# An explicit list schedule for every engine and DMA queue in a two-block transformer kernel

## The chip, the cores and the metric

The kernel runs on one core of a Trainium2 chip. The metric is device time of one execution in microseconds (us), the median of three runs. The engines named below are TensorE (PE, with PEld for its weight loads), VectorE (DVE), ScalarE (ACT), GpSimd (POOL) and SyncE (SP), whose queue issues most DMAs.

## The reference

Sequence length is 512 tokens, width 1024, one batch, all in float32. Five stages run one after the other on a residual stream `h`:

```
# layer A
q, k, v = split(rms_norm(h) @ a_w_qkv)              # 8 heads, two 64-wide halves each, v 128 wide
a       = softmax(q_c . k_c / 8 + t5_bias, causal)  # for each half c
o       = (a[0] - lam * a[1]) @ v
h      += (rms_norm(o) * (1 - lam_init)) @ a_w_o
h      += conv_gated_ffn(h);  h += ple(h)           # 2 x 2816 hidden; conv over 3 tokens
# layer B
k_nope, k_pe, v, q = latent projections, norms, rotary   # 16 heads, 128 + 64 wide
h      += causal_attention(q, k, v) @ b_w_o
h      += conv_gated_ffn(h);  h += ple(h)
# mixer: sparse attention (three branches), conformer convolution, chunked gated linear attention
z       = rms_norm(h) @ w_in
h      += concat(y_nsa, y_conv, y_gla) @ w_out
h      += (silu(x @ w_gate) * (x @ w_up)) @ w_down;  h += ple(h)
out     = rms_norm(h)
```

## The kernel before

All dense products are made of three: each float32 operand is split into a rounded high part and a rest, and `mm3` (L285 records every matmul) adds high x rest, high x high and rest x high in PSUM. A weight piece of 128 x 1024 values or less is loaded by SP into one of two raw buffers (`wr`, RB = 2, L378), ACT writes its high part `wh`, and DVE its rest `wl`, with a gain multiplied in where a norm stands ahead; four such pairs exist (`weight`, tags `wr`, `wh`, `wl`). `X` is the normed activation, transposed and split in the same way. PSUM has four `acc` banks for products over the weights, two `tr` banks for transposes and attention output, and two `s` banks for scores. L295 records every transpose, and L148 every operation on DVE, ACT and POOL.

Layer A works on two heads at a time: projections "p0 v0 p1 p2 p3 v1" (`A_ORDER`), the splits of q and k (`qs`, `kh`, `kl`) from `tr`, then for each head and 128-token tile the scores, a masked softmax (`sb`, `nm`), the transpose of the weights (`wT`) and the product with `v`. `sub_norm` normalizes attention output (`on`), and the last projection uses `a_w_o`. Layer B projects four groups of heads and runs attention per head; a bias row table (`rel_rows`, `tb` and `oh`, L537 on) for the mixer is made near its start. The mixer projects in `MIX_ORDER`, and the gated linear attention (tags `gst`, `gA`) walks its chunks in sequence. Each feed-forward stage holds the token tiles and streams the weights.

The order of work is set in two steps. Stages are coroutines that an `Order` object steps through by rank and by a rough clock (`Engine.slot`: 70 + 1.05 ns per word on DVE, 190 + 0.75 on ACT, 350 + 1.0 on POOL); that gives the order in which instructions are written. The framework's scheduler then orders each engine's instructions with its own timeline model (`schedule_with_timeline_sim=True` in `kernel`). The result is one fixed list of instructions for each engine.

Of the kernel before, what the change touches and what calls it, by code (L numbers as in the profile page):

```python
# [2 lines left out]

# [1 line left out]

# [6 lines left out]
F32 = mybir.dt.float32  # L12
# [20 lines left out]
FAC = 1.0  # L33
MIX_ORDER = "conv b gla k q0 kv a q1 q2 q3"
SL = 1.0
D = 1024
EPS = 1e-6
LAM_INIT = 0.8 - 0.6 * math.exp(0.0)
# [30 lines left out]
class Flag:  # L69


    def __init__(self):
        self.done = False
# [101 lines left out]
        self.used -= k  # L175


class Normed:


# [4 lines left out]
class Model:  # L185
    def __init__(self, ctx, tc, I, O):
        self.tc, self.I, self.O = tc, I, O
        self.n, self.rings = 0, {"acc": [], "tr": [], "s": []}
        self.od, self.g = Order(), {}
        nc = self.nc = Issue(self.od, tc.nc)  # L190
        self.acc, self.wu, self.xs, self.cr, self.sl = Slots(4), Slots(WB), Slots(2), Slots(3), Slots(2)
        pool = lambda name, **k: ctx.enter_context(tc.tile_pool(name=name, **k))
        self.cp = pool("cp", bufs=1)
        self.hp = pool("hp", bufs=1)
        self.wp = pool("wp", bufs=4)
        self.st = pool("st", bufs=4)
        self.sc = pool("sc", bufs=2)
        self.ps = pool("ps", bufs=2, space=bass.MemoryType.PSUM)
        self.dp = pool("dp", bufs=1, space=bass.MemoryType.DRAM)

        self.ident = self.cp.tile([P, P], F32, name="ident", tag="ident")
        make_identity(tc.nc, self.ident)
        self.mhalf = self.cp.tile([P, 32], F32, name="mhalf", tag="mhalf")
        nc.gpsimd.memset(self.mhalf, -0.5)
        self.h = self.hp.tile([P, NT, D], F32, name="h", tag="h")

        self.X = [self.hp.tile([P, 8, S], F32R, name=f"X{i}", tag=f"X{i}") for i in range(2)]
# [5 lines left out]
        return [y[:, k, c0:c0 + n] for y in self.X]  # L213

    def phase(self, name, bufs=1, **k):
        return self.tc.tile_pool(name=name, bufs=bufs, reuse_waits="tile", **k)

    def uid(self, s):
        self.n += 1
# [378 lines left out]
    def bias_a(self, B, fi):  # L598
# [5 lines left out]
        with self.phase("pos") as pp:  # L604
            T = lambda shape, dt, tag: pp.tile(shape, dt, name=self.uid(tag), tag=tag)
            parts = lambda raw, shape, tag="": self.pos_parts(T, raw, shape, tag)
            v = tc.nc.values_load(fi[0:1, 0:1], engines=[EV, EP, ES], min_val=0, max_val=1)
            thr = t5_thresholds()
            nc = self.tc.nc
            with tc.If(v != 0):  # L610
# [10 lines left out]
                for qt in range(NT):  # L621
# [10 lines left out]
                    for h0 in range(0, 8, 2):  # L632
                        for a in acc:
                            nc.vector.memset(a[:, :n], 0.0)
                        for b in range(32):
                            nc.vector.tensor_scalar(eq[:, :n], idx[:, :n], float(b), None, op0=ALU.is_equal)
                            for i, a in enumerate(acc):
                                nc.vector.scalar_tensor_tensor(
                                    a[:, :n], eq[:, :n], tab[:, b * 8 + h0 + i:b * 8 + h0 + i + 1], a[:, :n],
                                    op0=ALU.mult, op1=ALU.add)  # L640
                        for i, a in enumerate(acc):
                            nc.gpsimd.affine_select(
                                out=a[:, :n], in_=a[:, :n], pattern=[[-1, n]], base=qt * P,
                                channel_multiplier=1, compare_op=ALU.is_ge, fill=NEG)
                            nc.gpsimd.dma_start(self.skew(B[h0 // 2][qt + 1], 384 - qt * P, n)[i], a[:, :n])
        return v


# [1283 lines left out]
def model(ctx: ExitStack, tc: tile.TileContext, I, O):  # L1932
# [6 lines left out]
    def nxt(name):  # L1939
        def go(pp=None):  # L1940
# [11 lines left out]
    m.ffn_ple(*at["f2"], *m.glu_ffn(), g["ffn_norm_g_2", 0], I["p_2"][0][0], I["ple_w_gate_2"][0],  # L1952
              I["ple_w_proj_2"][0], g["ple_norm_g_2", 0], m.last_norm, "f2")
    m.od.run()


# [28 lines left out]
```

## Time and profile before

| quantity | value |
|---|---|
| median of three runs | 2270.28 us (2268.73 to 2272.74) |
| the profiled execution | 2270.06 us |
| its span in the trace | 2268.3 us |
| mean granted TensorE clock | 0.988 of full speed |
| PE, DVE, ACT, POOL busy | 97%, 59%, 47%, 8% of the span |

The span is 1.8 us shorter than the execution that it was taken from. Layer A lies at about 10 to 285 us, its feed-forward block at 285 to 684, layer B at 684 to 1140, its block at 1140 to 1482, the mixer at 1482 to 1881, and the last block from 1881 on. A stretch in which PE is busy without a gap can be shortened only by less work or a faster clock; a stretch with gaps can be shortened by giving PE something else to do, or by making what it waits for earlier.

### The profile page before, as it was taken

The page shows a single profiled execution, that of the slowest core. Times are in us where ns is not written, and L with a number is a line of the kernel's source. Part 1 is how long each engine was busy: PE and PEld are TensorE (multiplying, and loading weights), DVE is VectorE, ACT ScalarE, POOL GpSimd, SP SyncE. Part 2 cuts the span into 40 slices and gives each one's busy share as a digit, 9 for nine tenths or more (in the row PEclk, how much of TensorE's full clock was granted, in tenths as well). Part 3 has the DMA queues.
Part 4 walks back from the last instruction along what each step waited for, and adds up shares of the span by engine and source line. Part 5 has one row for each costly group of instructions (what it writes and reads, how often), then busy time and mean ns, then how long its engine had stood idle before and what let it go on. Part 6 is the DMA issues. An engine that isn't in the chain of part 4 may idle for free.

```text
span 2268.3 us, 30282 instructions
## 1 busy us (share of the span) xinstructions
PE 2197.4 (97%) x11166; PEld 1861.9 (82%) x11166; DVE 1336.6 (59%) x2885; ACT 1062.0 (47%) x2102; POOL 173.0 (8%) x232
## 2 busy tenths in 40 slices
PE   7987999999999999999999999999999999999998
PEld 5866798888887888888988888889978888888886
DVE  6668656446545777767565366357977643333344
ACT  4547445334444565555454254254657543323333
POOL 3123000000001121210000000001010000000000
PEclk9999999999999999999999999999989999999999
DMA  6323123332332412212133233234430123323322
GB/s 190 99 63 93 59 84 98 103 98 84 107 98 80 128 43 59 68 40 82 54 107 102 94 103 97 79 98 122 99 91 22 54 66 101 99 91 99 99 89 82
DMA packets 168839, 200.01 MB, mean 88 GB/s; under 512 B 19201, under 2 KB 123709, under 8 KB 168688
## 3 DMA queue, kind: packets, MB, share of 16 engines
q1 hardware_dynamic: 165172, 194.77, 28.1%
q10 hardware_dynamic: 2940, 2.02, 0.3%
q0 software_dynamic: 576, 1.26, 0.3%
q8 instruction: 88, 1.44, 0.3%
q14 instruction: 63, 0.52, 0.1%
HBM read 195.87 MB, written 7.38 MB: 90 GB/s over the span
## 4 chain that ended last, share of the span: by engine, by line
PE 91%; DVE 4%; ACT 1%; DMA 1%; issue 1%; POOL 0%; DVEq 0%; POOLq 0%; SPq 0%; ACTq 0%
PE acc L285 82%; PE s L285 4%; PE tr L295 4%; PE tr L285 1%; DVE wl L148 1%; DVE sb L148 1%; PE s L295 0%; DVE ss L148 0%; DVE X L148 0%; ACT wh L148 0%; DMA xn<-biasB 0%; DVE qs L148 0%; ACT wT L148 0%; DVE qn L148 0%; DMA tb<-rel_bias 0%
## 5 line engine op out<-in xcount | busy, mean ns | idle before, releaser
L285 PE MATMUL acc<-X,wh 128*128 128x512 f32 (+1 forms) x2592 | 734.9, 370 | 4.0 <-DVE X L148 4.0
L285 PEld LDWEIGHTS acc<-X,wh 128*128 128x128 f32 x2592 | 469.9, 189 | 85.0 <-DVE X L148 4.7
L285 PE MATMUL acc<-wh,X 128*128 128x512 f32 (+4 forms) x1664 | 502.0, 380 | 0.2 <-DVE X L148 0.2
L285 PE MATMUL acc<-X,wl 128*128 128x512 f32 (+1 forms) x1296 | 474.7, 369 | 0.0
L148 ACT ACTIVATE wh<-wr,gcol 128x512 fp32r<-128x512 f32 (+5 forms) x480 | 289.6, 656 | 208.4 <-PE acc L285 123.8
L148 DVE SCALAR_TENSOR_TENSOR wl<-wr,gcol,wh 128x512 fp32r<-128x512 f32 (+5 forms) x480 | 306.1, 674 | 131.5 <-ACT wh L148 129.5
L285 PEld LDWEIGHTS acc<-wh,X 128*128 128x128 f32 x1664 | 309.9, 190 | 45.9 <-DVE X L148 0.7
L285 PE MATMUL acc<-wl,X 128*128 128x512 f32 (+4 forms) x832 | 322.4, 388 | 7.3 <-DVE qn L148 3.3
L285 PEld LDWEIGHTS acc<-X,wl 128*128 128x128 f32 x1296 | 244.2, 189 | 40.8
L148 DVE TENSOR_TENSOR wl<-wr,wh 128x1024 fp32r<-128x1024 f32 (+1 forms) x134 | 152.5, 1144 | 183.8 <-ACT wh L148 183.6
L148 POOL TENSOR_TENSOR ss<-ss,mhalf 128x1 f32<-128x1 f32 (+3 forms) x140 | 128.9, 923 | 1727.4 <-DVE ss L148 1703.0
L148 ACT ACTIVATE wh<-wr 128x1024 fp32r<-128x1024 f32 (+1 forms) x134 | 132.5, 995 | 238.9 <-PE acc L285 191.2
L285 PE MATMUL acc<-wh,hh 128*128 128x512 f32 x528 | 205.7, 390 | 0.0
L285 PE MATMUL acc<-wl,hh 128*128 128x512 f32 x528 | 204.5, 389 | 0.0
L285 PE MATMUL acc<-wh,hl 128*128 128x512 f32 x528 | 203.7, 390 | 0.0
L285 PEld LDWEIGHTS acc<-wl,X 128*128 128x128 f32 x832 | 158.1, 190 | 32.8 <-DVE qn L148 3.6
L148 DVE SCALAR_TENSOR_TENSOR cv<-acc,cw,cv 128x511 f32<-128x511 f32 (+1 forms) x176 | 126.1, 745 | 95.2 <-ACT cv L148 94.4
L148 DVE TENSOR_TENSOR h<-h,acc 128x512 f32<-128x512 f32 x120 | 81.6, 684 | 61.3 <-PE acc L285 60.8
L285 PEld LDWEIGHTS acc<-wl,hh 128*128 128x128 f32 x528 | 99.1, 188 | 20.5
L285 PEld LDWEIGHTS acc<-wh,hl 128*128 128x128 f32 x528 | 99.1, 188 | 20.4
L285 PEld LDWEIGHTS acc<-wh,hh 128*128 128x128 f32 x528 | 99.1, 188 | 20.4
L148 ACT ACTIVATE wT<-tr 128x128 f32<-128x128 f32 (+3 forms) x160 | 68.8, 435 | 91.4 <-PE tr L295 90.6
(312 smaller groups left out, 2688.5 us busy)
## 6 DMA issues: line engine op xcount, KB each, us to landing
wr<-ffn_w_in SPq DMA_DIRECT2D x160, 256.0 KB
wr<-ffn_w_out SPq DMA_DIRECT2D x40, 512.0 KB
wr<-ple_w_gate SPq DMA_DIRECT2D x24, 512.0 KB
wr<-ffn_w_gate SPq DMA_DIRECT2D x40, 256.0 KB
wr<-ffn_w_up SPq DMA_DIRECT2D x40, 256.0 KB
wr<-ffn_w_down SPq DMA_DIRECT2D x20, 512.0 KB
wr<-a_w_qkv SPq DMA_DIRECT2D x32, 256.0 KB
wr<-b_w_o SPq DMA_DIRECT2D x16, 512.0 KB
```

Source lines behind the costliest of these rows:

```text
L148: return fn(*args, **kw)
L285: self.nc.tensor.matmul(out, lhsT=a, rhs=b, start=start, stop=stop)
L295: self.nc.tensor.transpose(out, src, self.ident[:src.shape[0], :src.shape[0]])
```

## The change

Every tile pool is wrapped so that each tile's pool and tag are known (`Pool`). After all instructions are traced, `Sequence.graph` builds a dependence graph over them: reads and writes of SBUF by overlapping boxes, PSUM by bank, buffer reuse by `share`. `cost` gives each instruction a time in which its engine is taken and a time until its result is there. `place` is list scheduling: it steps time forward, and whenever an engine is free it takes, of the instructions that are ready, the one with the lowest rank. A first pass ranks by the order as written; then twice (`PASSES = 2`) a pass backward over the program gives how late each instruction can begin, and a pass forward ranks by that. `run` chains each engine's instructions in the order found, by dependences without semaphores. What stands ahead of a branch in `bias_a` (the start of the program) keeps its order.

```diff
+    def cost(i, engine, dma, ins, outs):
+        words = lambda a: math.prod(n for _, n in a.ap[1:])
+        n = max([words(a) for a in ins + outs] or [1])
+        if dma:
+            return 410.0, 1700.0 + 2.1 * n
+        if engine == "PE":
+            n = words(ins[0])
+            f32 = ins[0].dtype == F32 and not any(a.tensor.name.startswith("ident") for a in ins)
+            if f32:
+                return max(223.0, n / 1.2 + 30.0), 175.0 + 1.66 * n
+            pitch = max(110.0, n / 2.4 + 13.6)
+            return pitch, pitch + 162.0
...
+    def place(self, ops, rank, back=False):
...
+            at, e = best
+            due(e, at)
+            k = heapq.heappop(now[e])[1]
+            (pitch, took), first, tab = ops[k][3], ops[k][5], ops[k][6]
+            if tab and tab != table and not back:
+                at, table = at + (1280.0 if table else 0.0), tab
+            free[e] = at + pitch
+            begin[k] = free[e] if back else at
+            order[e].append(k)
...
+    def run(self):
+        ops = self.graph()
+        order, begin = self.place(ops, range(len(ops)))
+        for _ in range(PASSES):
+            _, late = self.place(ops, [-t for t in begin], True)
+            order, begin = self.place(ops, [-t for t in late])
+        for e in self.ENGINES:
+            seq = [ops[k][0] for k in order[e] if not ops[k][5]]
+            for x, y in zip(seq, seq[1:]):
+                self.tc.add_manual_dep(y, x.name, mybir.DependencyInfo(
+                    mybir.DependencyClass.NoSync, mybir.DependencyReason.DATA), reason="order")
...
-        pool = lambda name, **k: ctx.enter_context(tc.tile_pool(name=name, **k))
+        pool = lambda name, **k: ctx.enter_context(self.sq.pool(name, **k))
...
     m.od.run()
+    m.sq.run()
```

The instructions themselves stay the same, but for ACT's table loads (15 in the order of before, 17 now, the two more in the mixer). Of PE's 10580 matmuls 5444 stand elsewhere, by 9 places on average and 213 at most; on SP 217 of 637 DMAs moved, by 1.6 places on average. In layer A the mean shift on PE is 22 to 42 places, in the mixer up to 32, and in the feed-forward blocks no move is over 24 places. The DVE order has a mean shift of 11 places; ACT's is nearly unchanged.

The line numbers of the changed kernel are larger (matmul L509, transpose L519, the helper L150). Three places follow; a number behind a name is one buffer.

PE in layer A before, at the end of the v1 projection (`acc_3762`): the transposes of the last q and k heads (`tr_3783`, `tr_3810`) stand behind it.

```order
L285 MATMUL acc_3762<-wh_3866,X_84 128x512
L295 MATMUL tr_3783<-ident,qn_3717 128x128 x4
L285 MATMUL s_3985<-kh_3013,qs_3012 128x512
L285 MATMUL s_3985<-kl_3014,qs_3012 128x512
L295 MATMUL tr_3810<-ident,qn_3751 128x128 x4
L295 MATMUL tr_3889<-ident,sb_3464 128x128
L295 MATMUL tr_3893<-ident,sb_3482 128x128
L285 MATMUL tr_3900<-v_3758,wT_3891 128x128
```

PE there now:

```order
L509 MATMUL acc_3759<-wh_3826,X_84 128x512
L519 MATMUL tr_3783<-ident,qn_3717 128x128 x4
L509 MATMUL acc_3760<-wl_3827,X_83 128x512
L509 MATMUL acc_3760<-wh_3826,X_83 128x512
L509 MATMUL acc_3760<-wh_3826,X_84 128x512
L509 MATMUL acc_3760<-wl_3827,X_83 128x512
```

The first transpose moved 73 places ahead, from 725 to 652, the second from 728 to 664, and the products of v1 (`acc_3759` to `acc_3762`) now stand between and behind them, up to row 749.

DVE in layer A before: `qs` and `kl` are the splits of those transposes, `wl_3965`, `wl_4332` and `wl_4338` weight splits for `a_w_o`, `on` and `ss` parts of `sub_norm`.

```order
L148 TENSOR_TENSOR wl_3965<-wr_3963,wh_3964 128x1024
L148 SCALAR_TENSOR_TENSOR kl_3425<-tr_3733,gcol_196,kh_3424 64x2x128
L148 TENSOR_TENSOR wl_4332<-wr_4330,wh_4331 128x1024
L148 SCALAR_TENSOR_TENSOR qs_3423<-tr_3783,gcol_196,qs_3423 64x2x128
L148 TENSOR_REDUCE ss_4000<-on_3998 128x4
L148 TENSOR_SCALAR ss_4000<-ss_4000 128x4
L148 TENSOR_TENSOR wl_4338<-wr_4336,wh_4337 128x1024
L148 SCALAR_TENSOR_TENSOR qs_3423<-tr_3810,gcol_196,qs_3423 64x2x128
L148 TENSOR_REDUCE ss_4014<-on_4012 128x4
L148 TENSOR_TENSOR on_3998<-o_2556,ss_4000 128x512
L148 SCALAR_TENSOR_TENSOR kl_3425<-tr_3783,gcol_196,kh_3424 64x2x128
L148 SCALAR_TENSOR_TENSOR kl_3425<-tr_3810,gcol_196,kh_3424 64x2x128
```

DVE there now:

```order
L150 SCALAR_TENSOR_TENSOR qs_3423<-tr_3810,gcol_196,qs_3423 64x2x128
L150 SCALAR_TENSOR_TENSOR qs_3423<-tr_3783,gcol_196,qs_3423 64x2x128
L150 SCALAR_TENSOR_TENSOR rat_3652<-z_3538,nlam,rz_3651 128x1
L150 TENSOR_REDUCE ss_4000<-on_3998 128x4
L150 SCALAR_TENSOR_TENSOR kl_3425<-tr_3810,gcol_196,kh_3424 64x2x128
L150 SCALAR_TENSOR_TENSOR kl_3425<-tr_3783,gcol_196,kh_3424 64x2x128
L150 SCALAR_TENSOR_TENSOR sb_3536<-sb_3536,rat_3652 128x256
L150 TENSOR_TENSOR on_3969<-o_2372,ss_3971 128x512
L150 SCALAR_TENSOR_TENSOR qs_3423<-tr_3810,gcol_196,qs_3423 64x2x128
L150 TENSOR_SCALAR ss_4000<-ss_4000 128x4
L150 TENSOR_TENSOR wl_3959<-wr_3957,wh_3958 128x1024
L150 SCALAR_TENSOR_TENSOR kl_3425<-tr_3810,gcol_196,kh_3424 64x2x128
```

The first split of `tr_3783` moved from 1954 to 1941, and its second `kl` from 1967 to 1959; of the weight splits `wl_3965` moved to 1969, `wl_4332` to 1995 and `wl_4338` to 2013.

PE at the start of layer B before: `tr_7988` and `tr_7991` are the two products of `rel_rows` with the table `tb`, `acc_8100` and `acc_8057` a projection.

```order
L285 MATMUL acc_8100<-wl_8051,X_83 128x320
L285 MATMUL acc_8100<-wh_8050,X_83 128x320
L285 MATMUL acc_8100<-wh_8050,X_84 128x320
L285 MATMUL tr_7988<-oh_7985,tb_7982 8x512
L285 MATMUL tr_7991<-oh_7985,tb_7982 8x128
L295 MATMUL tr_8143<-ident,xn_7900 128x128 x4
```

PE there now:

```order
L509 MATMUL acc_8100<-wh_8034,X_84 128x320
L509 MATMUL tr_7988<-oh_7985,tb_7982 8x512
L509 MATMUL acc_8100<-wl_8043,X_83 128x320
L509 MATMUL acc_8100<-wh_8042,X_83 128x320
L509 MATMUL acc_8100<-wh_8042,X_84 128x320
L509 MATMUL tr_7991<-oh_7985,tb_7982 8x128
L509 MATMUL acc_8100<-wl_8043,X_83 128x320
```

`tr_7988` now stands ahead of the last 12 products of `acc_8100` and not behind them. The DMA that fills `tb` stands at row 474 of ACT's order (470 before).

PE in the mixer before: the last projection of queries (`acc_16696`) ends, and small products of the gated linear attention and of the sparse attention follow without a projection until row 7278.

```order
L285 MATMUL acc_16696<-X_83,wh_16675 128x512
L285 MATMUL acc_16696<-X_83,wl_16676 128x512
L295 MATMUL tr_16631<-ident,cln 128x128 x2
L285 MATMUL acc_16715<-gst_15926,gq 128x256
L295 MATMUL tr_16636<-ident,cln 128x128 x2
L285 MATMUL s_16729<-hs_16169,w_16163 128x64 x2
L285 MATMUL s_16754<-w_16244,hs_16727 128x64 x4
L285 MATMUL tr_16712<-diag,gs_16007 128x512
L285 MATMUL tr_16717<-gv,gs_16083 128x256
```

PE there now:

```order
L509 MATMUL acc_16696<-X_84,wh_16675 128x512
L509 MATMUL acc_16696<-X_83,wh_16675 128x512
L509 MATMUL tr_16712<-diag,gs_16007 128x512
L509 MATMUL acc_16696<-X_83,wl_16676 128x512
L509 MATMUL acc_16696<-X_84,wh_16675 128x512
L509 MATMUL acc_16696<-X_83,wh_16675 128x512
L509 MATMUL tr_16717<-gv,gs_16083 128x256
L509 MATMUL acc_16696<-X_83,wl_16676 128x512
L509 MATMUL acc_16715<-gst_15926,gq 128x256
L509 MATMUL acc_16696<-X_84,wh_16675 128x512
L509 MATMUL acc_16696<-X_83,wh_16675 128x512
```

The products of `acc_16696` are spread between the small ones, from row 7136 to 7199; rows 7200 to 7282 still hold no projection.

## Rows read from the trace of the kernel before

**Rows 1.** The page: busy us of each engine, share, instructions

```profile
PE 2197.4 (97%) x11166; PEld 1861.9 (82%) x11166; DVE 1336.6 (59%) x2885; ACT 1062.0 (47%) x2102; POOL 173.0 (8%) x232
```

**Rows 2.** Windows: stretch, its us, busy us (instructions) per engine, granted clock, DMA share, GB/s

```profile
0.00:57.00 57.00, 41.09 (x193) 31.96 (x194) 36.59 (x81) 27.16 (x50) 22.28 (x27) 1.00 0.63 189
57.00:285.00 228.00, 201.47 (x1019) 166.12 (x1018) 160.69 (x431) 124.10 (x290) 44.98 (x52) 0.95 0.26 78
171.00:228.00 57.00, 45.83 (x232) 37.39 (x232) 49.54 (x125) 40.37 (x93) 19.16 (x23) 0.91 0.32 93
285.00:684.00 399.00, 399.00 (x1888) 334.97 (x1887) 220.17 (x321) 173.12 (x261) 4.88 (x8) 1.00 0.31 96
684.00:741.00 57.00, 52.86 (x257) 44.18 (x256) 31.84 (x69) 24.77 (x49) 8.44 (x14) 0.97 0.28 80
741.00:1140.00 399.00, 394.78 (x2292) 345.30 (x2292) 280.59 (x795) 220.27 (x506) 65.00 (x74) 1.00 0.23 69
1140.00:1482.00 342.00, 342.00 (x1523) 283.43 (x1522) 185.04 (x264) 141.66 (x212) 2.20 (x4) 1.00 0.31 98
1482.00:1539.00 57.00, 54.68 (x277) 46.17 (x276) 31.71 (x52) 28.35 (x47) 7.54 (x22) 1.00 0.35 108
1539.00:1881.00 342.00, 333.84 (x2050) 297.05 (x2049) 238.16 (x659) 193.00 (x484) 13.30 (x24) 0.98 0.26 72
1881.00:2223.00 342.00, 342.00 (x1527) 283.52 (x1526) 128.65 (x182) 113.78 (x173) 2.20 (x4) 1.00 0.31 98
2223.00:2280.00 57.00, 35.69 (x158) 29.23 (x156) 23.12 (x40) 15.82 (x32) 2.21 (x4) 0.94 0.15 56
```

**Rows 3.** The chain of waits: start us, us, what

```profile
330.11 332.78 PE acc L285 x1468
...
730.85 4.32 DMA tb<-rel_bias
```

**Rows 4.** Timeline of PE: start us, us, instruction, idle before and its releaser

```profile
208.31 0.60 PE L295 MATMUL tr<-ident,qn 128*128 128x128 f32 x4
217.40 0.85 PE L295 MATMUL tr<-ident,sb 128*128 128x128 f32 x2 [8.48 <-DVE kl L148]
```

**Rows 5.** Timeline of DVE at the same place

```profile
207.82 1.23 DVE L148 TENSOR_TENSOR wl<-wr,wh 128x1024 fp32r<-128x1024 f32 x1 [1.37 <-ACT wh L148]
...
214.92 0.89 DVE L148 SCALAR_TENSOR_TENSOR qs<-tr,gcol,qs 64x256 fp32r<-64x256 f32 x2
...
216.76 0.90 DVE L148 SCALAR_TENSOR_TENSOR kl<-tr,gcol,kh 64x256 fp32r<-64x256 f32 x2
```

**Rows 6.** Windows of 10 us

```profile
210.00:220.00 10.00, 2.60 (x9) 2.16 (x10) 8.88 (x20) 6.11 (x15) 4.07 (x6) 0.58 0.33 106
1570.00:1580.00 10.00, 10.00 (x53) 9.25 (x52) 10.00 (x28) 6.56 (x18) 0.00 (x0) 1.00 0.53 150
1680.00:1690.00 10.00, 8.91 (x40) 6.84 (x39) 8.89 (x45) 4.12 (x17) 1.29 (x2) 0.64 0.00 0
1690.00:1700.00 10.00, 9.09 (x35) 7.00 (x36) 6.06 (x31) 5.10 (x20) 1.32 (x2) 0.68 0.01 2
```

**Rows 7.** Timeline of PE at the start of layer B

```profile
731.51 0.46 PE L285 MATMUL acc<-wh,X 128*128 128x320 f32 x2
...
731.95 0.46 PE L285 MATMUL acc<-wh,X 128*128 128x320 f32 x2
735.31 1.23 PE L285 MATMUL tr<-oh,tb 33*8 33x512 f32 x4 [2.90 <-DMA tb<-rel_bias]
```

**Rows 8.** ACT's table loads

```profile
L148 ACT ACT_TABLE_LOAD x15 | 19.2, 1283 | 1.6 <-PEq L1975 1.4
```

**Rows 9.** Waits of PE: us in total, times, longest

```profile
PE s L285 <- DVE nm L148: 6.9, 11, 1.6
```

**Rows 10.** Timeline of PE in layer B, score products

```profile
909.17 1.02 PE L285 MATMUL s<-kT,qT 128*128 128x512 f32 x2
...
910.50 0.81 PE L285 MATMUL s<-kT,qT 128*128 128x384 f32 x2
```

More of the change, by code (lines that the diff above doesn't have):

```diff
@@ L1 @@
+import heapq
 import math
-from contextlib import ExitStack
+from contextlib import ExitStack, contextmanager
 import numpy as np
@@ L35 @@
 SL = 1.0
+PASSES = 2
 D = 1024
@@ L188, in __init__ @@
         self.n, self.rings = 0, {"acc": [], "tr": [], "s": []}
-        self.od, self.g = Order(), {}
+        self.od, self.g, self.sq = Order(), {}, Sequence(tc)
         nc = self.nc = Issue(self.od, tc.nc)
         self.acc, self.wu, self.xs, self.cr, self.sl = Slots(4), Slots(WB), Slots(2), Slots(3), Slots(2)
-        pool = lambda name, **k: ctx.enter_context(tc.tile_pool(name=name, **k))
+        pool = lambda name, **k: ctx.enter_context(self.sq.pool(name, **k))
         self.cp = pool("cp", bufs=1)
@@ L215, in phase @@
     def phase(self, name, bufs=1, **k):
-        return self.tc.tile_pool(name=name, bufs=bufs, reuse_waits="tile", **k)
+        return self.sq.pool(name, bufs=bufs, reuse_waits="tile", **k)
     def uid(self, s):
@@ L606, in bias_a @@
             parts = lambda raw, shape, tag="": self.pos_parts(T, raw, shape, tag)
+            at = len(self.sq.traced())
             v = tc.nc.values_load(fi[0:1, 0:1], engines=[EV, EP, ES], min_val=0, max_val=1)
@@ L645, in bias_a @@
                             nc.gpsimd.dma_start(self.skew(B[h0 // 2][qt + 1], 384 - qt * P, n)[i], a[:, :n])
+        self.sq.parts = at, len(self.sq.traced())
         return v
```

155 lines of the change are left out of this document (added).

## The prediction

> **What bounds the kernel now.** I read the busy times first: PE is busy for 2197.4 of 2268.3 us [rows 1], so all the gaps on PE together are 70.9 us, and the change takes no work away from PE. Then I read windows cut at the stages [rows 2], where the reader is to see in which stages the gaps lie. The three feed-forward blocks (285 to 684, 1140 to 1482, 1881 to 2223) have PE busy for all of 399, 342 and 342 us at full clock: 1083 us without a gap. Their 399 us hold 1888 matmuls, 211 ns each, and the chain of waits goes 332.78 us through products alone [rows 3]. The gaps are: 15.9 us in the first 57; 26.5 in layer A (228.00 less 201.47); 4.1 at the passage into layer B (57.00 less 52.86); 4.2 in layer B; 2.3 at the passage into the mixer (57.00 less 54.68); 8.2 in the mixer; 9.6 behind 2223 (45.3 to the span's end, less 35.69). They add up to 70.8.
>
> The granted clock adds something. Over layer A its mean is 0.95, over the mixer 0.98 [rows 2]. If all of the missing share fell on busy time, it would be 228 x 0.05 = 11.4 us and 342 x 0.02 = 6.8. So layer A can give at most 26.5 + 11.4 = 38 us, and the mixer at most 8.2 + 6.8 = 15.
>
> Third, the timeline of the longest gap. PE finishes transposes of q and k from 208.31 and starts nothing until 217.40; 8.48 us of that end with DVE's split `kl` [rows 4]. DVE works through it, but among the splits that PE waits for stands a weight split of 1.23 us for the projection by `a_w_o`, which PE reaches much later [rows 5]. [...] So in layer A PE waits for DVE, which is busy for 70% of the stretch (160.69 of 228) and in the fullest 57 us for 87% (49.54) [rows 2]. DVE has the time, but spends some of it on the wrong instruction first.
>
> **The change part by part.** No instruction of work is added or removed, so every gain is a gap filled and every loss a gap opened. The sum is made against the profiled execution, 2270.06 us, which is 0.2 us under the median of the runs; 1.8 us of it lie outside the span.
>
> Layer A, the largest term. On PE the transposes of the last q and k heads move from rows 725 and 728 to 652 and 664, and v1's products spread between attention up to row 749; on DVE `wl_3965`, `wl_4332` and `wl_4338` now stand behind the splits for which PE waited. This takes away the 8.48 us gap and fills others of the same kind, because PE has a product ready beside almost each transpose. What is late next is DVE itself: its 160.69 us of work stay in this stage, or wait for it. If DVE were as full all along as in its fullest 57 us (87%), the stage would last 185 us, 43 less, more than the 38 that PE can give. If only the one stall goes, it is 8.5. I take the middle of DVE's two shares, 79%: 160.69 / 0.787 = 204 us, a gain of 24; ends 8 and 38.
>
> Of these 24 some is clock and not idle time. The clock stood at 0.58 while PE stood still and was at 1.00 in the blocks without a gap [rows 6, 2]. [...] Idle time alone would cap the stage at 26.5 and not at 38.
>
> Mixer. Of the 15 us, 8.8 lie in 1680 to 1700: 2.0 idle, and 20 x 0.34 = 6.8 of clock (0.64 and 0.68) [rows 6]. There PE has only small products of the chunked linear attention, with 40 and 35 matmuls in 10 us; at 1570 it has 53 in its 10.00 busy us. The new order spreads `acc_16696` between these small products, but rows 7200 to 7282 still hold no projection, and the chain from chunk to chunk is as long as before. So I take 6 of 15, about two thirds of the 8.8. The two added table loads are 2 x 1.283 = 2.6 us on ACT [rows 8]; ACT is busy for 193.00 of 342 us in this stage [rows 2], which hides them, and without that cover they cost all 2.6. Ends: 15 and -3.
>
> Passage into layer B. PE waits 2.90 us for the DMA that fills `tb`, which took 4.32 us from its issue [rows 7, 3]. The new plan reckons 1.7 + 0.0021 x 8 = 1.72 us for it, so it puts `tr_7988` ahead of the last 12 products of `acc_8100` and not behind them. From 731.51 to 731.95 PE starts three such products, 0.147 us each [rows 7]; 12 of them are 1.8 us of work that now stands behind the waiting matmul. The fill DMA itself stands no earlier on ACT. So this place gets 0 to 1.8 us worse; it would get 2.9 better if the DMA landed as planned. I take -1.
>
> [...]
>
> The other places: 0. In layer B PE is busy for 394.78 of 399 us [rows 2], and what moves there is products past other products; ends +4 and what the slower rival says. In the feed-forward blocks no move is over 24 places. DVE is busy for 55% of the first block (220.17 of 399), so weight splits come in time with room. The first 57 us keep their order up to the branch, and the chain behind the last matmul consists of the same instructions. On SP the loads wait for a free raw buffer and not for their row, so that 217 DMAs moved by 1.6 places count as nothing; without that cover a load comes later by a row or two. POOL is busy for 173.0 us of the span [rows 1] and bounds nothing.
>
> Sum: 24 + 6 - 1 = 29, so 2270.06 - 29 = 2241 us.
>
> **The rivals.** First, another wait takes the place of the one removed. DVE is at 87% in the worst 57 us and does the same work afterwards, and attention needs DVE's softmax for each head and tile in its order. Then layer A gives its 8.5 us, the mixer 2, and `tb` takes 1: 2270 - 9.5 = 2260.5. For it: PE stands still just where DVE is fullest. Against it: DVE ran at 10.00 of 10 us at 1570 with PE at 10.00 beside it [rows 6], so a full DVE need not stop PE.
>
> Second, the schedule fills nearly everything: layer A 38, mixer 15, layer B 4, that is 2270 - 57 = 2213. For it: the plan works on dependences, on the whole program at once. Against it: it would ask DVE for 85% of layer A (160.69 / 190), and the linear attention's chain for time that is not there.
>
> Third, slower, in layer B. The plan prices a 512-wide float32 score product at 512 / 1.2 + 30 = 457 ns, so the pair (`kT`, `kpeT`) at 0.91 us. In the trace the next score product starts 1.33 us behind the first of a pair, 910.50 less 909.17 [rows 10]. PE thus runs behind its plan at each head and tile, while the products that served as filler have moved: `acc_9919` and `acc_10820` of this layer, which stood within 19 rows each, now have pieces 150 rows further on. If each of the 16 x 4 heads and tiles then waits for its softmax as scores now do where they wait (6.9 us in 11 times, 0.63 us each [rows 9]), that is 64 x 0.63 = 40 us, more than the 29, and the time is 2281. It decides from 29 / 64 = 0.45 us for each. Against it: PE behind its plan means that DVE and ACT are early, and there is next to no gap in this stage now.
>
> Fourth, the change does not do what it says for the engine that bounds: products trade places with products, while the order of waits stays, and the time is 2270. Against it stand the moved rows of layer A.
>
> **How the numbers follow.** The forecast has 0.47, with its own range 2228 to 2253. The first rival has 0.24 (2254 to 2268), the second 0.12 (2206 to 2228), the third 0.11, the fourth 0.06. What a measurement of this kernel can tell from no change is 0.2%, 4.5 us, so faster means below 2265.7. Faster: 0.47 + 0.12 + 0.21 of the first rival's 0.24 = 0.80. Same: the other 0.03, and 0.05 of the fourth's 0.06, 0.08 in all. Slower: 0.11 and 0.01, that is 0.12. The range from 2212 to 2271 leaves out about half of the second rival at the low end, 0.06, and the slower cases at the high end, 0.12.
>
> **What the profile of the changed kernel would show.** If the forecast is right, the stretch from 57 us to the end of layer A is about 24 us shorter, with DVE's share near 79% and a clock nearer 1.00 there, and no PE wait of 8 us for `kl` is left. The three blocks keep 399 and 342 us without a gap. The pair at `tb` waits 2.9 to 4.7 us. The first rival shows as the same DVE work in the same stretch, with waits for `nm`, `ss` or `on` in place of `kl`; the third as PE waits in layer B for `nm`, some 64 of them. The prediction is wrong in its kind if the gain comes from another stage than layer A, or if a feed-forward block opens gaps.

## The result and the profile after

The changed kernel takes 2215.22 us (median of 4 runs, 2214.55 to 2220.53) beside 2269.51 us before: a ratio of 0.9764, 95% interval 0.9745 to 0.9782. The forecast was 2241 us in a range of 2212 to 2271. The time lies in the range and the direction is right, but the gain is 54 us where 29 were forecast, and the time is outside the forecast's own 2228 to 2253. The second rival, which had 0.12, said 2213.

The profiled execution has a span of 2212.8 us, 55.5 less than before. PE is busy for 2175.8 us of it, 21.6 less than in [rows 1] with the same 11166 matmuls. This is the view of windows that begin and end at nearly the same places of the work (the numbers of matmuls say how nearly), columns as in [rows 2]:

```profile
57.00:250.00 193.00, 189.90 (x1022) 158.96 (x1021) 160.03 (x428) 124.99 (x286) 44.56 (x49) 1.00 0.33 98
250.00:649.00 399.00, 399.00 (x1891) 335.17 (x1890) 219.39 (x323) 173.47 (x263) 6.17 (x9) 1.00 0.31 96
649.00:699.00 50.00, 49.01 (x234) 40.04 (x232) 28.09 (x56) 21.09 (x40) 7.64 (x11) 1.00 0.28 81
699.00:1098.00 399.00, 395.77 (x2311) 345.05 (x2309) 279.85 (x805) 223.25 (x512) 69.34 (x78) 1.00 0.23 70
1098.00:1440.00 342.00, 342.00 (x1528) 283.61 (x1528) 185.31 (x267) 142.75 (x215) 2.57 (x4) 1.00 0.32 97
1440.00:1497.00 57.00, 56.28 (x282) 47.33 (x281) 30.90 (x50) 29.11 (x48) 4.69 (x11) 1.00 0.36 112
1497.00:1826.00 329.00, 325.23 (x2042) 290.64 (x2042) 241.27 (x660) 193.15 (x486) 18.11 (x35) 0.99 0.27 75
1826.00:2168.00 342.00, 342.00 (x1527) 283.61 (x1526) 130.16 (x184) 114.59 (x175) 2.57 (x4) 1.00 0.32 98
```

The three blocks again have no gap in 399, 342 and 342 us. Layer A shrank from 228 to 193 us. Its gaps fell from 26.5 to 3.1 us (193.00 less 189.90), and its busy time from 201.47 to 189.90, since the clock stands at 1.00 and not at 0.95. That makes 23.4 of idle time and 11.6 of clock. The window at the start of layer B holds fewer matmuls than the one of before (234 and 257), so it is read together with the next: the two shrank from 456 to 449 us (2549 and 2545 matmuls). The mixer with the window ahead of it shrank from 399 to 386 (2327 and 2324).

For a sharper division I take the times at which the same work begins or ends, from the answers for three tiles: the first product with `hh` (behind layer A), the last with `oxh` (end of layer B), the last transpose of `praw` (behind the mixer). Before:

```profile
L285 PE MATMUL acc<-wl,hh x528: 389/389/395, 425.6 to 2200.8; 128*128 128x512 f32 x176
```

```profile
L285 PE MATMUL acc<-wh,oxh x64: 387/389/481, 952.9 to 1107.2; 128*128 128x512 f32 x64
```

```profile
L295 PE MATMUL tr<-ident,praw x24: 270/272/273, 315.2 to 1878.0; 128*128 128x128 f32 x24
```

After:

```profile
L509 PE MATMUL acc<-wl,hh x528: 389/389/477, 391.1 to 2147.1; 128*128 128x512 f32 x176
```

```profile
L509 PE MATMUL acc<-wh,oxh x64: 387/389/477, 911.3 to 1065.5; 128*128 128x512 f32 x64
```

```profile
L519 PE MATMUL tr<-ident,praw x24: 270/272/277, 276.8 to 1823.5; 128*128 128x128 f32 x24
```

"First and last start" are the two numbers behind the durations. The first `hh` product came at 425.6 and now comes at 391.1; the last `oxh` product at 1107.2, now 1065.5; the last `praw` transpose at 1878.0, now 1823.5. So the work up to the first gained 34.5 us, layer B with its passage 41.7 - 34.5 = 7.2, the mixer 54.5 - 41.7 = 12.8, and the tail 55.5 - 54.5 = 1.0. The table gives these stretches for every run, in us (the one called layer B begins at the first `hh` product and so holds most of the first block, the mixer's holds the second, the rest the third; the blocks' own time does not change); the median and the ratio come from the timed runs (each ratio against the kernel before as it ran beside, 2268.13 to 2270.48 us), the stages from the profiled one. Stages that an experiment leaves alone lie within 2.2 us of the changed kernel's.

| kernel | median | ratio | to first hh | layer B | mixer | rest |
|---|---|---|---|---|---|---|
| before | 2269.51 | | 425.6 | 681.6 | 770.8 | 390.3 |
| changed | 2215.22 | 0.9764 (0.9745 to 0.9782) | 391.1 | 674.4 | 758.0 | 389.3 |
| PE's order alone | 2281.20 | 1.0049 (1.0032 to 1.0065) | 407.4 | 696.5 | 784.7 | 390.9 |
| the other engines' alone | 2313.53 | 1.0191 (1.0174 to 1.0208) | 436.7 | 696.2 | 789.0 | 391.4 |
| rank as written | 2252.80 | 0.9926 (0.9909 to 0.9942) | 393.9 | 688.7 | 777.6 | 390.6 |
| rough durations | 2225.69 | 0.9807 (0.9791 to 0.9823) | 399.3 | 673.1 | 763.7 | 389.3 |
| v1 in one piece | 2230.72 | 0.9827 (0.9811 to 0.9844) | 406.4 | 676.2 | 757.8 | 390.2 |
| and weight splits first | 2234.01 | 0.9844 (0.9827 to 0.9860) | 409.5 | 674.3 | 759.1 | 389.2 |
| last queries in one piece | 2224.09 | 0.9806 (0.9785 to 0.9827) | 389.3 | 673.7 | 766.8 | 389.7 |
| DVE + 32 | 2218.23 | 0.9768 (0.9753 to 0.9783) | 392.5 | 673.8 | 760.2 | 389.6 |
| DVE + 64 | 2233.97 | 0.9849 (0.9832 to 0.9865) | 411.1 | 673.1 | 758.3 | 389.1 |
| float32 price | 2211.53 | 0.9742 (0.9727 to 0.9757) | 390.2 | 671.4 | 756.1 | 390.4 |
| and DMA price | 2217.53 | 0.9761 (0.9747 to 0.9774) | 393.1 | 674.5 | 758.8 | 389.1 |
| and five passes | 2216.35 | 0.9762 (0.9749 to 0.9775) | 389.8 | 674.8 | 759.4 | 390.2 |

PE's waits in layer A are nearly gone. The view of waits over 57 to 251 us has four lines (us in total, times, longest):

```profile
PE tr L519 <- DVE o L150: 0.8, 1, 0.8
PE s L509 <- DVE nm L150: 0.7, 1, 0.7
PE tr L519 <- DVE kl L150: 0.7, 2, 0.4
PE tr L519 <- DVE gcol L150: 0.6, 1, 0.6
```

The 8.48 us for `kl` of [rows 4] have become 0.7 in two waits, and nothing took their place. Over the whole span the waits for `nm` of [rows 9] are now:

```profile
PE s L509 <- DVE nm L150: 1.1, 2, 0.7
```

Two are left of eleven.

At the start of layer B the wait for `tb` did not grow but all but went away. The timeline of PE and the chain of waits:

```profile
697.15 1.01 PE L509 MATMUL tr<-oh,tb 33*8 33x512 f32 x2 [0.17 <-DMA tb<-rel_bias]
```

```profile
693.98 3.03 DMA tb<-rel_bias
```

PE waits 0.17 us and not 2.90 [rows 7]. The DMA took 3.03 us where it had taken 4.32 [rows 3], and PE came to it later: 3.0 us behind the start of the DMA's piece (697.15 - 0.17 - 693.98) and not 1.6 (735.31 - 2.90 - 730.85).

### The profile page after: what moved, and what is told of

Same layout as the page of the kernel before. It is cut to its first block, busy times and chain, and to the rows that moved or that the text cites. A ratio compares the mean times of both kernels' runs of the same rounds, so it can differ in the third digit from the quotient of the medians.

```text
span 2212.8 us, 30322 instructions
## 1 busy us (share of the span) xinstructions
PE 2175.8 (98%) x11166; PEld 1844.9 (83%) x11166; DVE 1333.9 (60%) x2885; ACT 1065.1 (48%) x2104; POOL 177.8 (8%) x232
## 4 chain that ended last, share of the span: by engine, by line
PE 91%; DVE 4%; DMA 1%; ACT 1%; issue 1%; POOL 0%; SPq 0%; DVEq 0%; POOLq 0%; ACTq 0%
PE acc L509 80%; PE s L509 5%; PE tr L519 4%; PE tr L509 1%; DVE wl L150 1%; PE s L519 0%; DVE ss L150 0%; DVE kl L150 0%; POOL ss L150 0%; DVE qs L150 0%; DVE X L150 0%; ACT xn L150 0%; DVE sb L150 0%; DMA wr<-b_w_dq 0%; DVE xn L150 0%
## 5 line engine op out<-in xcount | busy, mean ns | idle before, releaser
L509 PE MATMUL acc<-X,wh 128*128 128x512 f32 (+1 forms) x2592 | 736.3, 369 | 1.7 <-DVE X L150 1.7
L509 PEld LDWEIGHTS acc<-X,wh 128*128 128x128 f32 x2592 | 469.0, 189 | 82.5 <-DVE X L150 2.4
L509 PE MATMUL acc<-wh,X 128*128 128x512 f32 (+4 forms) x1664 | 503.4, 380 | 0.0
L509 PE MATMUL acc<-X,wl 128*128 128x512 f32 (+1 forms) x1296 | 477.4, 369 | 0.0
L150 ACT ACTIVATE wh<-wr,gcol 128x512 fp32r<-128x512 f32 (+5 forms) x480 | 291.2, 656 | 185.8 <-PE acc L509 131.1
L150 DVE SCALAR_TENSOR_TENSOR wl<-wr,gcol,wh 128x512 fp32r<-128x512 f32 (+5 forms) x480 | 306.0, 674 | 112.9 <-ACT wh L150 111.2
L509 PEld LDWEIGHTS acc<-wh,X 128*128 128x128 f32 x1664 | 307.6, 188 | 42.5 <-issue 0.5
L509 PE MATMUL acc<-wl,X 128*128 128x512 f32 (+4 forms) x832 | 322.6, 389 | 3.5 <-ACT X L150 1.8
L509 PEld LDWEIGHTS acc<-X,wl 128*128 128x128 f32 x1296 | 244.1, 189 | 41.1 <-DVE wl L150 0.3
L150 POOL TENSOR_TENSOR ss<-ss,mhalf 128x1 f32<-128x1 f32 (+3 forms) x140 | 133.6, 955 | 1714.3 <-DVE ss L150 1664.2
L150 DVE TENSOR_TENSOR wl<-wr,wh 128x1024 fp32r<-128x1024 f32 (+1 forms) x134 | 152.6, 1143 | 176.5 <-ACT wh L150 176.0
L150 ACT ACTIVATE wh<-wr 128x1024 fp32r<-128x1024 f32 (+1 forms) x134 | 132.4, 993 | 232.6 <-PE acc L509 188.3
L509 PE MATMUL acc<-wl,hh 128*128 128x512 f32 x528 | 205.9, 390 | 0.0
L509 PE MATMUL acc<-wh,hh 128*128 128x512 f32 x528 | 205.4, 389 | 0.0
L509 PE MATMUL acc<-wh,hl 128*128 128x512 f32 x528 | 204.8, 389 | 0.0
L150 DVE SCALAR_TENSOR_TENSOR cv<-acc,cw,cv 128x511 f32<-128x511 f32 (+1 forms) x176 | 124.7, 745 | 120.4 <-ACT cv L150 120.3
L509 PEld LDWEIGHTS acc<-wl,X 128*128 128x128 f32 x832 | 156.7, 188 | 27.5 <-ACT X L150 2.7
L150 ACT ACTIVATE cv<-acc,cw 128x512 f32<-128x512 f32 x88 | 65.7, 777 | 122.8 <-PE acc L509 122.3
L509 PEld LDWEIGHTS acc<-wh,hl 128*128 128x128 f32 x528 | 99.1, 188 | 20.7
L509 PEld LDWEIGHTS acc<-wh,hh 128*128 128x128 f32 x528 | 99.1, 188 | 20.4
L509 PEld LDWEIGHTS acc<-wl,hh 128*128 128x128 f32 x528 | 99.1, 188 | 20.3
L150 DVE TENSOR_TENSOR h<-h,acc 128x512 f32<-128x512 f32 x120 | 81.7, 685 | 55.1 <-PE acc L509 54.0
```

The source lines that it names most:

```text
L150: return fn(*args, **kw)
L509: self.nc.tensor.matmul(out, lhsT=a, rhs=b, start=start, stop=stop)
```

## The experiments

**Which engine's order carries the gain.** Two kernels chain a part of the engines only; the framework's scheduler orders the others against it.

```diff
-        for e in self.ENGINES:
+        for e in ("PE",):              # PE's order alone
-        for e in self.ENGINES:
+        for e in self.ENGINES[1:]:     # the other engines' order alone
```

> Only PE's instructions are chained, in exactly the order of the changed kernel; the framework's scheduler orders DVE, ACT, POOL and SP against it with its own model, as it did before. Theory 1 (the order on PE, a projection product beside almost every transpose, carries the gain): 2215 to 2232 us, first product with hh near 391 to 400 us (425.6 before, 391.1 changed). Theory 2 (the order on DVE, urgent splits first, carries it): 2240 to 2262 us, first product with hh after 408 us.

> DVE, ACT, POOL and SP are chained in the order of the changed kernel, PE is left to the framework's scheduler. Theory 1 (PE's order carries the gain): 2240 to 2262 us. Theory 2 (DVE's order carries it): 2215 to 2232 us. If both orders are needed together, this and the run with PE's chain alone both lie above 2240 us.

Both are slower than before, 2281.20 and 2313.53 us. Neither theory holds; the third case written down for the second run does, both above 2240 us. Over the whole kernel the order of one part is worth nothing where the framework's scheduler orders the rest. PE's order alone keeps half of layer A's gain (first `hh` at 407.4) and loses 14.9 us in layer B and 13.9 in the mixer against before. With PE's order alone the waits of layer A, over 57 to 267 us, are for DVE:

```profile
PE tr L519 <- DVE kl L150: 3.9, 3, 1.6
PE tr L519 <- DVE rat L150: 2.6, 2, 2.3
PE tr L519 <- DVE o L150: 1.5, 1, 1.5
```

With the other engines' order alone, over 57 to 296 us, PE waits for DVE and ACT:

```profile
PE acc L509 <- DVE qn L150: 6.8, 4, 2.3
PE tr L519 <- DVE o L150: 4.5, 6, 2.1
PE tr L509 <- ACT wT L150: 3.3, 3, 2.5
```

I read this as PE standing before operands whose makers come at another place in DVE's or ACT's order than PE's order reckons with. A rival is left open: the framework's scheduler may do worse when a part of the order is given to it than when it is free, and no run separates the two.

**Lateness, and the durations.** One kernel keeps the list scheduling and ranks by the order as written; one keeps lateness and takes the rough durations of before.

```diff
-PASSES = 2
+PASSES = 0
```
```diff
-            if f32:
-                return max(223.0, n / 1.2 + 30.0), 175.0 + 1.66 * n
...
+            took = max(1.687 * n, 213.0) if f32 else max(0.4217 * n, 107.0)
...
+            fixed, word = {"Activation": (190.0, 0.75), "Pool": (350.0, 1.0)}.get(engine, (70.0, 1.05))
+            took = fixed + word * n
+        return took, took + LAT
```

> The same list scheduling with the same durations, but each engine takes of what is ready the instruction that was written first (PASSES = 0), not the one that can begin least late. Theory 1 (lateness decides: splits for later projections must give way): 2240 to 2265 us. Theory 2 (that an engine takes what is ready, by fair durations, is enough): 2213 to 2225 us.

> The same scheduling, lateness included, but with the rough durations that the kernel before used where it writes its instructions (70 + 1.05 n on DVE, 190 + 0.75 n on ACT, 350 + n on POOL, 0.42 n on PE, 200 ns until a result is there; DMAs as in the change). Theory 1 (list scheduling by lateness is what gains, durations only have to be fair): 2213 to 2225 us. Theory 2 (the gain rests on durations fitted to the chip): 2230 to 2260 us.

Ranked as written, the kernel takes 2252.80 us, within theory 1's bounds: about 17 us of the 54 are kept. By stages this splits. Layer A keeps 31.7 of its 34.5 us, so there lateness is not what matters, against theory 1. In layer B and the mixer it is slower than before (688.7 and 777.6 beside 681.6 and 770.8), and lateness is worth 14.3 and 19.6 us. In this kernel PE still waits 3.2 us for `tb` at the start of layer B. With rough durations the kernel takes 2225.69 us, 0.7 over theory 1's upper bound: 44 of 54 us are kept, and fitted durations are worth about 10. (The profiled execution is 12.6 us over the changed kernel's: 8.2 in layer A, 5.7 in the mixer, and 1.3 less in layer B.)

**Filler on PE in layer A.** In PE's chain the products of v1 stand in one piece again, ahead of the transpose `tr_3783`; the next kernel also puts the four weight splits for `a_w_o` ahead of the last splits of q and k, on ACT and DVE. (The weight splits were not moved alone: with v1 spread, its products still hold the buffers that they would write.)

```diff
+            if e == "PE":
+                at = next(j for j, x in enumerate(seq) if self.wrote(x) == "tr412")
+                v1 = [x for x in seq[at:] if self.wrote(x) in ("acc405", "acc406", "acc407", "acc408")]
+                moved = {x.name for x in v1}
+                seq = seq[:at] + v1 + [x for x in seq[at:] if x.name not in moved]
```

The next kernel has this besides:

```diff
+            if e in ("DVE", "Activation"):
...
+                for wl, wh, tr in (("wl437","wh436","tr412"),("wl440","wh439","tr412"),("wl553","wh552","tr413"),("wl556","wh555","tr413")):
+                    x = next(x for x in seq if self.wrote(x) == (wl if e == "DVE" else wh))
+                    at = next(j for j, y in enumerate(seq) if tr in reads(y))
+                    if seq.index(x) > at:
+                        seq.remove(x)
+                        seq.insert(at, x)
```

> PE's chain of the changed kernel with one place undone: the products of v1 that stood among attention pieces stand in one piece ahead of the transpose of the last but one q and k tile, as before the change; the other engines keep the changed order. Theory 1 (the filler on PE decides at this place): PE stands still there for some us again, with a lower granted clock, and the time is 6 to 12 us over the changed kernel, 2221 to 2227 us. Theory 2 (the order on DVE decides, since urgent splits still come first): 0 to 3 us over it.

> As the run with v1 in one piece, and on ACT and DVE the four weight splits for the projection by a_w_o moved ahead of the splits of the last two q and k tiles, as before the change (4.9 us of DVE work). Theory 1 (filler on PE decides): 0 to 2 us over the run with v1 in one piece. Theory 2 (the weight splits in front of the urgent ones decide): 5 us or more over it.

The one place on PE costs 15.5 us (2230.72), and 15.3 of them lie ahead of the first `hh` product (406.4 beside 391.1). That is theory 1's side, but over its 6 to 12. Windows of 10 us of this kernel show how it comes about:

```profile
180.00:190.00 10.00, 10.00 (x46) 8.28 (x45) 0.00 (x0) 0.00 (x0) 0.00 (x0) 1.00 0.16 53
190.00:200.00 10.00, 3.93 (x21) 2.96 (x19) 5.93 (x19) 6.46 (x14) 2.69 (x5) 0.92 0.18 52
200.00:210.00 10.00, 6.28 (x18) 3.88 (x18) 9.12 (x21) 5.68 (x14) 4.08 (x3) 0.50 0.33 105
210.00:220.00 10.00, 9.18 (x43) 7.45 (x44) 7.90 (x21) 7.03 (x17) 0.00 (x0) 0.72 0.06 14
```

From 180 to 190 PE runs 46 products of v1, and DVE and ACT have 0.00 us of work. DVE's timeline shows what it waits for, the split `qs` of a transpose that stands behind v1:

```profile
193.85 0.48 DVE L150 SCALAR_TENSOR_TENSOR qs<-tr,gcol,qs 64x256 fp32r<-64x256 f32 x1 [14.99 <-ACT qs L150]
```

Then PE has 3.93 and 6.28 us of work in 10, and the clock falls to 0.50. So this piece of filler, in the wrong place, cost twice: DVE stood still for 14.99 us while PE used the filler up, and then PE waited for DVE, 6.5 us for `kl` in two waits. The changed kernel has work on both engines in the same stretch:

```profile
180.00:190.00 10.00, 10.00 (x49) 8.12 (x49) 9.68 (x25) 7.77 (x17) 4.46 (x6) 1.00 0.41 113
190.00:200.00 10.00, 9.17 (x53) 7.49 (x51) 7.71 (x23) 5.70 (x14) 1.85 (x1) 1.00 0.30 98
200.00:210.00 10.00, 9.82 (x63) 8.27 (x61) 9.93 (x28) 8.70 (x21) 1.01 (x1) 1.00 0.22 67
```

This is not quite the place as it was before the change. There DVE had other work while PE ran v1:

```profile
190.00:200.00 10.00, 10.00 (x50) 8.26 (x49) 7.60 (x20) 6.30 (x14) 3.67 (x5) 1.00 0.37 107
200.00:210.00 10.00, 8.91 (x44) 7.20 (x42) 8.39 (x13) 6.93 (x12) 2.76 (x5) 1.00 0.34 105
```

So the 15.5 us are the price of v1 in one piece beside orders of the others that reckon with v1 spread; what the filler alone was worth in the kernel before is not shown.

The weight splits in front cost 3.3 us more (2234.01), 3.1 of them in layer A: between the theories' bounds, and the intervals of the two ratios overlap. Two of the four weight splits ran (from 181.98 us on) while DVE had nothing else to do, so the run does not show what they cost in the kernel before, where DVE was busy. In these two kernels most of the stall is PE's order.

**Filler in the mixer.** The products of each of the last two query projections stand in one piece.

```diff
+                for q3 in ("acc2692", "acc2715"):
+                    at = next(j for j, x in enumerate(seq) if self.wrote(x) == q3)
+                    one = [x for x in seq[at:] if self.wrote(x) == q3]
+                    moved = {x.name for x in one}
+                    seq = seq[:at] + one + [x for x in seq[at:] if x.name not in moved]
```

> PE's chain of the changed kernel with one place of the mixer undone: the products of each of the last two query projections stand in one piece, from where their first stands, and the small products of the two attentions follow without projections between; the other engines keep the changed order. Theory 1 (projection products between the small ones keep the clock up): a stretch of 10 to 20 us there with a granted clock near 0.65, and 4 to 9 us over the changed kernel, 2219 to 2224 us. Theory 2 (the mixer's gain is from the order of the other engines): 0 to 2 us over it and the clock at 1.00.

2224.09 us, 8.9 over the changed kernel, and the mixer takes 8.8 more (766.8 beside 758.0): theory 1. The profiled execution is only 6.7 over the changed kernel's, since the stages ahead of the mixer came out 2.5 us shorter. (Before the change only the second of the two stood in one piece, so this undoes a little more than the change did.) The clock falls again at this place, in this kernel first and then in the changed one:

```profile
1630.00:1640.00 10.00, 8.21 (x51) 6.76 (x50) 7.95 (x35) 5.79 (x17) 0.31 (x1) 0.98 0.01 3
1640.00:1650.00 10.00, 9.83 (x32) 7.45 (x32) 7.67 (x33) 5.92 (x20) 1.50 (x2) 0.50 0.21 52
1650.00:1660.00 10.00, 9.69 (x49) 7.21 (x49) 7.32 (x40) 6.98 (x28) 0.00 (x0) 0.83 0.00 1
```

```profile
1630.00:1640.00 10.00, 10.00 (x70) 8.89 (x68) 8.85 (x45) 7.06 (x20) 1.50 (x2) 1.00 0.25 55
1640.00:1650.00 10.00, 8.07 (x41) 6.39 (x41) 7.92 (x36) 6.09 (x21) 0.31 (x1) 0.83 0.00 0
1650.00:1660.00 10.00, 9.29 (x54) 7.03 (x54) 9.21 (x40) 7.96 (x33) 1.15 (x1) 1.00 0.00 1
```

With the queries in one piece PE is busy for 9.83 of 10 us with 32 matmuls at 0.50, behind 10 us in which it was busy for 8.21; the changed kernel has 8.07 busy us with 41 at 0.83. So the filler keeps most of the clock, but a stretch without projections is left.

**How full DVE can be.** In layer A the rest of k alone (32 instructions), and the rests of q and k (64), are written twice. The values stay the same. The line for k:

```diff
+                            nc.vector.scalar_tensor_tensor(kl[a, c, :, ts], pt[a, 2:4], kg[a],
+                                                           kh[a, c, :, ts].bitcast(F32), op0=ALU.mult,
+                                                           op1=ALU.subtract)
```

> In layer A each split of q and k heads writes its rest twice (64 more DVE instructions on the path from the transposes, 0.45 us each from the trace of before, 29 us of DVE work; the values stay the same), and the schedule is made anew. In the changed kernel DVE is busy for about 84% of 57 to 251 us. Theory 1 (layer A is now bound by PE, DVE has room): 0 to 8 us over the changed kernel, 2215 to 2223 us. Theory 2 (layer A is bound by DVE, as the forecast had it, only at a higher share): 20 to 29 us more, 2235 to 2244 us.

> In layer A only the rest of k is written twice (32 more DVE instructions, 0.48 us each, 15 us of DVE work; values unchanged), scheduled anew. The run with 64 more cost 18.7 us for 31 us of work, with DVE at 89% of the stage. Theory 1 (DVE has room up to a ceiling near 89% and then each us of its work costs one): 160.9 + 15.4 = 176 us fit into 194 us at 91%, so 0 to 6 us over the changed kernel, 2215 to 2221 us. Theory 2 (every added us costs 0.6 from the first on): 8 to 11 us over it, 2223 to 2226 us.

32 more instructions, 15.3 us of DVE work, move the first `hh` product by 1.4 us (392.5) and the time by 3.0, neither clear of noise: theory 1 of that run. 64 more, 30.8 us, move it by 20.0 (411.1) and the time by 18.8, which lies between the two theories of that run. So the first half of the added work costs next to nothing, and the second about its own length (15.7 us by the medians, 18.6 by the first `hh` product). The windows of the stage, changed kernel, 32 more, 64 more:

```profile
57.00:251.00 194.00, 190.90 (x1027) 159.75 (x1026) 160.86 (x430) 125.20 (x287) 44.59 (x50) 1.00 0.32 97
```

```profile
57.00:251.00 194.00, 190.54 (x1015) 158.00 (x1014) 168.77 (x455) 123.48 (x285) 45.10 (x50) 1.00 0.32 97
```

```profile
57.00:271.00 214.00, 202.28 (x1047) 166.20 (x1046) 189.18 (x495) 126.27 (x292) 47.77 (x51) 0.98 0.30 91
```

DVE's share is 83% (160.86 of 194), 87% and 88% (189.18 of 214), and with 88% PE has gaps and a clock of 0.98. With 32 more the stage holds only 7.9 us more of DVE's work (168.77 less 160.86) and 25 instructions more, so some other work has moved out of it. And the mean over the stage hides a stretch where DVE is all but full. These are the windows from 107 to 207 us, in the same order:

```profile
107.00:207.00 100.00, 96.90 (x513) 79.66 (x512) 89.01 (x235) 71.18 (x165) 33.45 (x38) 1.00 0.33 98
```

```profile
107.00:207.00 100.00, 96.81 (x507) 78.99 (x506) 93.83 (x257) 69.54 (x162) 32.78 (x37) 1.00 0.29 88
```

```profile
107.00:207.00 100.00, 93.02 (x464) 74.46 (x462) 95.68 (x244) 63.45 (x143) 32.20 (x35) 1.00 0.29 88
```

For 100 us DVE worked at 94% and PE lost nothing to the changed kernel (96.81 and 96.90 us); at 96% PE fell behind. So 88% is the highest mean seen, and not shown to be a limit. The added instructions also lengthen the way from each transpose to the scores, and no run separates that from DVE's share.

**Other prices.** A longer float32 price; with it each DMA 1.0 us longer; with both, five passes. The longer price is 0.87 us for 512 columns and so 1.75 for the pair (`kT`, `kpeT`), where the plan had 0.91 and [rows 10] show 1.33: it errs as far on the other side.

```diff
-                return max(223.0, n / 1.2 + 30.0), 175.0 + 1.66 * n
+                return max(223.0, 1.687 * n + 10.0), 175.0 + 1.687 * n
-            return 410.0, 1700.0 + 2.1 * n
+            return 410.0, 2700.0 + 2.1 * n
-PASSES = 2
+PASSES = 5
```

> The change with one price corrected from the trace: a float32 matmul of n columns takes 1.69 n + 10 ns of PE and not n / 1.2 + 30 (512 columns: 0.87 us and not 0.46). Theory 1 (layer B has next to no gap, so that a wrong price there costs nothing): within 3 us of the changed kernel, 2212 to 2218 us. Theory 2 (wrong prices put products in the wrong places): 4 to 10 us less, 2205 to 2211 us.

> As the run with the float32 price, and each DMA reckoned 1.0 us longer (2.7 us and 2.1 ns a word), nearer to the 4.3 us that the small table took. Theory 1 (weights are there long before they are needed): within 3 us of the run with the float32 price. Theory 2 (the plan counts on DMAs that land later): 3 us or more below it.

> As the run with both prices, with five passes in place of two. Theory 1 (the order has settled after two): within 2 us of it. Theory 2: some us less.

The float32 price gives 2211.53 us, 3.7 less than the changed kernel, just beyond theory 1's bound and short of theory 2's; the intervals of the ratios overlap (0.9727 to 0.9757 and 0.9745 to 0.9782), so that it is better is likely and not settled. 3.0 of it lie in layer B, and there at its start and not among the score products. From 690 to 720 and from 720 to 1060 us, the changed kernel first, then the one with the float32 price:

```profile
690.00:720.00 30.00, 26.22 (x157) 22.19 (x156) 24.81 (x90) 18.56 (x48) 8.85 (x12) 1.00 0.61 184
720.00:1060.00 340.00, 339.56 (x1927) 293.47 (x1926) 239.11 (x701) 189.59 (x444) 64.23 (x70) 1.00 0.20 60
```

```profile
690.00:720.00 30.00, 29.10 (x168) 24.58 (x167) 27.07 (x95) 18.06 (x48) 8.09 (x12) 1.00 0.67 194
720.00:1060.00 340.00, 339.60 (x1929) 293.26 (x1929) 237.91 (x698) 192.20 (x447) 63.89 (x71) 1.00 0.19 58
```

Behind 720 PE stands still for 0.4 of 340 us in both. The longer DMA price does not help: 2217.53 us, 6.0 more, which neither theory had (the intervals of the two ratios overlap). Five passes change nothing beyond noise: theory 1. The version with the float32 price has the lowest median of all that ran.

## Why the prediction was right in direction and half in size

**What bounds the kernel.** Right. The blocks gave nothing, all but 1.0 us of the gain came from the gaps and the clock in the stages named, and the two caps, 38 us for layer A and 15 for the mixer, held: 34.5 and 12.8 were gained.

**Layer A, the mis-sized term.** The term that was mis-sized is 24 us, where 34.5 were gained, and the step to it is "I take the middle of DVE's two shares, 79%". DVE's share was taken for the limit, and it was none at that height. The stage ran at 83%, and with 32 instructions more at 87% for next to no cost. Even at 87% the 160.9 us of DVE work need 185 us, less than the 190 us of work that PE has there: PE is the bound, and the gain goes near the cap. The forecast's own row pointed there: DVE at 10.00 of 10 us beside a full PE [rows 6]. The sentence that stood against the second rival, that "it would ask DVE for 85% of layer A", describes what happened.

The gain's split into idle time and clock was right: 23.4 and 11.6 us beside caps of 26.5 and 11.4. The slow clock of layer A came behind PE's waits (0.58 from 210 to 220 us, with the wait of 8.48 us [rows 6, 4]), and it went with them (1.00 from 57 to 250 us). What makes the clock fall, no run shows. In the mixer it fell without a long wait: with the last queries in one piece the clock stood at 0.50 behind 10 us in which PE was busy for 8.21, and from 1600 to 1660 us no wait of PE was longer than this one:

```profile
PE tr L529 <- DVE gst L150: 1.1, 1, 1.1
```

The mechanism was right in part. The 8.48 us stall went, as forecast. But the stall is only a part of the stage's gain: from 210 to 220 us PE stood still for 7.40 us and its clock lacked up to 4.2 [rows 6], at most some 12 of the 38 us; the rest was spread over the stage. The forecast told the stall as a matter of DVE's order, with PE's filler second. The run with v1 in one piece brings a like stall back by PE's order alone, and the weight splits add 3 us to it, within the noise. But PE's order alone made the whole kernel slower than before, so it is not a matter of one engine, and how the 34.5 us divide between the engines' orders stays open.

**The mixer.** 12.8 us and not 6. At the place that was named the forecast was about right. These lines of it hold, before the change, 3.9 us of idle time (40.00 less 36.09) and lack up to 6.8 of clock (40 x 0.17), and after it 2.6 and 1.8:

```profile
1670.00:1710.00 40.00, 36.09 (x180) 27.50 (x178) 31.87 (x141) 26.48 (x91) 3.24 (x6) 0.83 0.09 26
```

```profile
1640.00:1660.00 20.00, 17.36 (x94) 13.42 (x94) 17.13 (x74) 14.05 (x53) 1.46 (x2) 0.91 0.00 0
```

That is up to 6.3 us gained, and some 4 are left where rows 7200 to 7282 hold no projection. The other half came from places for which nothing was counted. The largest is this one before the change, 2.9 us of idle time and up to 1.7 of clock, near the stage's end:

```profile
1830.00:1840.00 10.00, 7.06 (x43) 6.58 (x42) 7.92 (x15) 6.63 (x12) 1.10 (x2) 0.83 0.35 107
```

**Passage into layer B.** Wrong in sign: -1 was forecast, and the passage with layer B gave 7.2. The wait for `tb` went from 2.90 to 0.17 us. The order was read rightly, but not the time: PE came to the waiting matmul 1.4 us later behind the DMA's start, and the DMA landed 1.3 us sooner; why it did, no run separates. The forecast also left out the clock behind this wait. Before, the stretch from 730 to 750 us held 4.5 us of idle time and lacked up to 3.4 of clock; the changed kernel has 3.8 us of idle time from 690 to 720, at a clock of 1.00. This is the line of before:

```profile
730.00:750.00 20.00, 15.52 (x81) 13.18 (x80) 13.47 (x59) 8.71 (x26) 2.67 (x4) 0.83 0.65 192
```

So this place gave about 4 of the 7.2 us: the wait and its slow clock went, and some waits of other kinds came. The plan's 1.72 us for this small table is below both of its landings, 4.32 and 3.03 us on ScalarE's queue. Nor would a DMA that landed as planned have given the whole 2.9 us back, as the forecast has it: by an estimate from these numbers, a landing 2.6 us sooner than the 4.32 [rows 3] leaves 0.3 of the 2.90 us in the old order, and more where PE comes earlier.

**The rivals.** The second came nearest: it said 2213 for 2215, with 38, 15 and 4 us where 34.5, 12.8 and 7.2 were gained. Its reason, a plan by dependences over the whole program, fits what the runs show, though none tests it by itself. Another wait in place of the one removed: no, the waits of layer A sum to 2.8 us. Slower in layer B: the price of the score products is off by 0.42 us a pair, but it costs nothing there, since PE has 0.4 us of gaps in the 340 us from 720 on. It opens no waits for `nm` either: PE waited 6.9 us for them before [rows 9], and waits 1.1 now, of which 0.7 lie in layer A. That the change does nothing for the engine that bounds: no.

## What to carry to other kernels

Price a new order by each stage's cap, its idle time on the bounding engine and what its clock lacks, and then ask what really limits the stage: compare each other engine's work, at the share that it reaches where it is fullest, with the bounding engine's own work. A middle between two shares is no limit. And an order is one thing over all engines: a part of the good order, with the rest left to the framework's scheduler, was slower than the old order of all.

## What was not expected

A greedy list by the order as written gave layer A 31.7 of its 34.5 us, yet lost 7.1 in layer B and 6.8 in the mixer against before. Fitted durations were worth only some 10 us of the 54, and making one of them longer (DMA, by 1.0 us) did not help: 2217.53 beside 2211.53, with intervals that overlap. DVE kept PE fed at a share of 87% over the stage, and of 94% for 100 us of it, at a cost within the noise; the next 15 us of work cost about their own length.
